# A hybrid encoder step: expert picks turned later and two more tiles whole, keys rotated before they are scaled, two reorderings in the front

## The chip, the cores and the metric

The kernel runs on one core of one Trainium2 chip. It is one program of 33,129 instructions on five engines: TensorE (PE; its weight loads are listed apart as PEld), VectorE (DVE), ScalarE (ACT), GpSimd (POOL) and SyncE (SP, which here only issues transfers). The metric is the device time of one execution in microseconds (us). Lower is better.

## The reference, cut to what matters

One layer for 384 tokens: one prompt of 256, and eight samples of 16 tokens each. What the change touches is the query and key part of the sparse attention and the expert layer.

```python
def _dsa(P_dsa, pos, k_pos, cache_k, cache_v, cache_kidx, q_norm_w, k_norm_w):
    q, k, v, qi, ki, wi = _split(P_dsa, [ATT_W, ATT_W, ATT_W, IDX_HEADS * IDX_DIM, IDX_DIM, IDX_HEADS])
    q = _rope(_rmsnorm(hs(q), q_norm_w), pos)        # 16 heads of 64
    k = _rope(_rmsnorm(hs(k), k_norm_w), pos)
    ...
    o = _sparse_attend(q, qi, wi, pos, k_all, v_all, ki_all, k_pos)

def _peer(h, w_pq, peer_keys, peer_u, peer_v):       # 16384 experts, 128 x 128 keys
    q = (hb @ w_pq).reshape(PEER_BLOCK, PEER_HEADS, 2, PEER_DHALF)
    s = einsum('nhpd,hpkd->nhpk', q, peer_keys)
    s1, i1 = top_k(s[:, :, 0], 16);  s2, i2 = top_k(s[:, :, 1], 16)
    sc, j = top_k(s1[..., :, None] + s2[..., None, :], 16)     # 16 experts per head and token
    g = softmax(sc)
    act = gelu(einsum('nhkd,nd->nhk', peer_u[e], hb))
    return einsum('nhk,nhkd->nd', g * act, peer_v[e])
```

Around these stand a modulation of the layer by a matrix `w_ada`, an RWKV branch with a state per head, two gates, and projections. All is float32.

## The kernel before

The program is written in the order of its stages, and a scheduler that runs when the program is built then sets one fixed order of instructions for each engine, from its own estimate of durations; on the chip each engine goes through its list in order and waits at the semaphores that stand in it. Another edit of the program can so move instructions far from the edit.

**The front (0 to about 718 us).** After the modulation's head and the norm, `run` goes through the letters of `ORDER`: R is a pair of RWKV heads (`rwkv_pair`, a long chain of small steps on all engines, among them y L845 to L676), M a unit of the modulation matrix (`mod_unit`: two loads of 512 KB of `w_ada`, 8 matmuls of full width), G a unit of the gates (`gate_unit`), D a quarter of the attention (`dsa_quarter`: keys, queries and values of four heads, attention of the samples in `attend_s` and of the prompt in `attend_p`). M and G are the filling for the chains of R and D on PE. The weights that need float32 precision are split in two rounded parts, `wh` by ACT (L230) and `wl` by DVE (L234), and multiplied in three matmuls.

In a quarter, `nat3` copies the 128x768 keys (then queries) out of PSUM to `qx`, ACT squares them (L947, into the buffer `rpt`), DVE sums (L949), `rstd` takes the power on POOL (L436), DVE scales `qx` in place (L951), and `rope` rotates: two half-size multiplies on POOL into `rpt` (L877, L878), one full-size multiply and one add on DVE into `qr` (L880, L881). Then PE turns the result (L959), and the key result is also written out (L955). `index` calls the same `rope` three times. PSUM has eight banks: `mm` two, `fx` two, `dx` two, `bx` and `cp` one each. All of `attend_p` is in the two `dx` banks.

**The mix (708 to 840 us)** reads the two branches back from DRAM into the tiles `px` (L1171), which take over memory of the front, splits them into `pbh` and `pbl` and multiplies.

**The experts' front (842 to 1290 us).** `peer_select` makes the picks of three groups of 128 tokens on DVE: group 0 for the sparse way, groups 1 and 2 for the dense way. At its end for groups 1 and 2, three transposes of the picks `pix` and the weights `pg` go to one `dx` bank (L1384) and are copied to `pT1`, `pT2`. In the same time PE goes through the tiles of `peer_u` in `dense_u`: the first `N1` of 128 unsplit, in float32 (8 matmuls of 256 columns, each of which the trace shows as two), in turn in the `mm` and `fx` banks; the tiles after those split, with 24 matmuls each. The sparse way (`peer_sparse`) gathers 1 MB a round (L1573, a ring of three buffers) and computes on DVE with the result (raw L1580, then acc L1586, with two small steps on ACT between); `pull` sets how many rounds are written beside a tile. `weights` takes `pT1`, `pT2` apart into digits (L1424 to L1427), makes one-hot factors on DVE and ACT, and multiplies them on PE (`mm<-oh`).

**Dense v (1290 to 1757 us)** multiplies with all of `peer_v`, loaded once.

## Time and profile before

| | us |
|---|---|
| median of 3 runs | 1762.96 |
| lowest, highest | 1759.18, 1770.17 |
| the profiled execution's own time | 1759.49 |
| its span, first to last instruction | 1757.7 |
| mean granted clock of PE | 0.981 |

The span is what all rows of the trace add up to; the profiled execution's own time has 1.8 us around it, and the median lies 3.5 us above that execution. A share of busy time is the mean over stages that are limited by different things, so a stage is read from its own window.

### The profile page before, as it was taken

What the parts mean: (1) busy time and instruction counts of PE and PEld (TensorE: products, weight loads), DVE (VectorE), ACT (ScalarE), POOL (GpSimd) and SP (SyncE); (2) the same over time, 40 slices, a digit from 0 to 9 for tenths busy, and PEclk for the clock granted to TensorE, in tenths of its full rate; (3) what the DMA queues carried; (4) which work ended last, traced back from release to release, by engine and by line L of the source; (5) the groups of instructions that cost most, each with busy time, mean ns of one, the idle gap of its engine ahead of it and who ended that gap; (6) DMA issues with size and microseconds to landing.
All of it is one profiled execution on the core that took longest, in us unless ns stands there. A gap on an engine that the chain in (4) does not pass through costs nothing.

```text
span 1757.7 us, 33129 instructions
## 1 busy us (share of the span) xinstructions
PE 1679.5 (96%) x12392; PEld 1410.2 (80%) x12392; DVE 1353.6 (77%) x2907; ACT 747.5 (43%) x1666; POOL 550.5 (31%) x616
## 2 busy tenths in 40 slices
PE   6999899999999999999998999999999999999998
PEld 4988788777888877899887889999976667767766
DVE  4448878778867765556999998899957778778787
ACT  4533343334342333335323255578853433443344
POOL 2433343333333421024032233342243224323232
PEclk8999899999999999999999999999999999999999
DMA  8543662555365365765488999997569999999996
GB/s 305 161 123 101 187 194 68 145 166 174 94 197 161 94 207 189 246 193 171 144 334 313 358 333 366 397 340 238 179 251 381 348 346 376 375 349 391 349 379 216
DMA packets 172537, 436.71 MB, mean 248 GB/s; under 512 B 46036, under 2 KB 86100, under 8 KB 155992
## 3 DMA queue, kind: packets, MB, share of 16 engines
q1 hardware_dynamic: 153944, 300.36, 50.8%
q0 software_dynamic: 18432, 134.23, 19.7%
q8 instruction: 98, 1.61, 0.4%
q14 instruction: 63, 0.52, 0.1%
HBM read 403.23 MB, written 31.30 MB: 247 GB/s over the span
## 4 chain that ended last, share of the span: by engine, by line
PE 55%; DVE 19%; DMA 11%; issue 8%; ACT 3%; POOL 2%; SPq 1%; DVEq 0%; POOLq 0%; ACTq 0%
PE mm L226 21%; PE fx L226 10%; PE dx L226 10%; PE cp L226 6%; PE bx L226 6%; DMA raw<-in_puv,pe 3%; DVE wl L234 3%; DVE raw L1580 2%; DVE acc L1586 2%; DMA w<-in_puT 2%; DMA w<-in_pv 2%; ACT wh L230 1%; DMA w<-in_w_in 1%; DVE TX L698 1%; DMA NL<-d 1%
## 5 line engine op out<-in xcount | busy, mean ns | idle before, releaser
L234 DVE TENSOR_TENSOR wl<-w,wh 128x1024 fp32r<-128x1024 f32 (+1 forms) x276 | 345.8, 1260 | 109.0 <-ACT wh L230 71.3
L230 ACT ACTIVATE wh<-w 128x1024 fp32r<-128x1024 f32 (+1 forms) x284 | 296.6, 1050 | 163.7 <-PE mm L226 74.3
L1573 POOL DMA_INDIRECT raw<-in_puv,pe x128 | 173.6, 1356 | 423.4 <-PE dx L226 155.4
L226 PE MATMUL fx<-h2h,wl 128*128 128x256 f32 x704 | 200.1, 285 | 8.2 <-DVE wl L234 8.0
L226 PE MATMUL fx<-h2h,wh 128*128 128x256 f32 x704 | 200.6, 285 | 1.4 <-ACT wh L230 1.1
L226 PE MATMUL fx<-h2l,wh 128*128 128x256 f32 x704 | 197.4, 281 | 0.0
L1586 DVE SCALAR_TENSOR_TENSOR acc<-raw,dots,acc 128x1024 f32<-128x1024 f32 x127 | 166.1, 1308 | 14.8 <-ACT dots L1582 14.8
L1580 DVE SCALAR_TENSOR_TENSOR raw<-raw,sh 128x1024 f32<-128x1024 f32 x128 | 158.9, 1241 | 14.0 <-DMA raw<-in_puv,pe 13.8
L226 PEld LDWEIGHTS fx<-h2h,wl 128*128 128x128 f32 x704 | 132.7, 189 | 12.3 <-DVE wl L234 11.5
L226 PEld LDWEIGHTS fx<-h2h,wh 128*128 128x128 f32 x704 | 132.6, 188 | 6.4 <-ACT wh L230 3.6
L226 PEld LDWEIGHTS fx<-h2l,wh 128*128 128x128 f32 x704 | 132.9, 189 | 1.6 <-issue 1.1
L226 PE MATMUL mm<-LTh,wh 128*128 128x384 f32 (+2 forms) x352 | 123.4, 351 | 1.4 <-ACT wh L230 0.8
L226 PE MATMUL mm<-LTl,wh 128*128 128x384 f32 (+2 forms) x352 | 123.1, 350 | 0.9 <-POOL LTl L488 0.9
L226 PE MATMUL mm<-LTh,wl 128*128 128x384 f32 (+2 forms) x352 | 122.4, 348 | 0.0
L226 PE MATMUL mm<-h2f,w 128*128 128x256 f32 x448 | 104.0, 385 | 0.0
L226 PE MATMUL mm<-wh,LTh 128*128 128x256 f32 x336 | 100.3, 299 | 2.9 <-ACT qx L888 2.9
L1581 ACT ACTIVATE dots<-dots 128x1 f32<-128x1 f32 x128 | 25.6, 200 | 177.0 <-DVE raw L1580 176.5
L226 PE MATMUL mm<-wl,LTh 128*128 128x256 f32 x336 | 99.4, 296 | 0.0
L226 PE MATMUL mm<-wh,LTl 128*128 128x256 f32 x336 | 98.6, 293 | 0.0
L226 PEld LDWEIGHTS mm<-h2f,w 128*128 128x128 f32 x448 | 85.0, 192 | 12.2 <-issue 0.2
L226 PE MATMUL fx<-h2f,w 128*128 128x256 f32 x320 | 73.8, 383 | 0.0
L226 PEld LDWEIGHTS mm<-LTh,wh 128*128 128x128 f32 (+2 forms) x352 | 66.5, 189 | 7.1 <-issue 3.0
(577 smaller groups left out, 4235.0 us busy)
## 6 DMA issues: line engine op xcount, KB each, us to landing
w<-in_puT SPq DMA_DIRECT2D x128, 512.0 KB, 7.1
w<-in_pv SPq DMA_DIRECT2D x128, 512.0 KB, 6.6
w<-in_w_in SPq DMA_DIRECT2D x70, 512.0 KB, 4.5
w<-in_w_ada SPq DMA_DIRECT2D x48, 512.0 KB, 4.8
cKT<-in_cKT SPq DMA_DIRECT2D x32, 256.0 KB, 4.3
cV<-in_cV SPq DMA_DIRECT2D x32, 256.0 KB, 4.5
w<-in_w_pq SPq DMA_DIRECT2D x16, 512.0 KB, 4.2
d<-wst SPq DMA_DIRECT2D x8, 832.0 KB, 4.3
```

What stands on the lines that cost most here:

```text
L226: return self.nc.tensor.matmul(out, l, r, start=start, stop=stop, skip_group_check=True, **kw)
L230: self.nc.scalar.activation(hi, src, AF.Copy)
L234: (self.nc.vector if eng == "v" else self.nc.gpsimd).tensor_tensor(lo, src, hi, op=OP.subtract)
L698: nc.vector.tensor_tensor(X[:, :t, :t], T[:, :t, :t].rearrange("p s c -> p c s"), NL[:, :t, t].unsqueeze(1).to_broadcast([48, t, t]), op=O ...
L1573: d = nc.gpsimd.indirect_dma_start(out=bass.AP(tensor=u.tensor, offset=u.offset, ap=[u.ap[0], [1, 2048]]), out_offset=None, in_=self.I["puv"],
L1580: nc.vector.scalar_tensor_tensor(u, u, 1.0, h2, op0=OP.mult, op1=OP.mult, accum_out=dot)
L1581: nc.scalar.activation(dot, dot, AF.Gelu_apprx_tanh)
L1586: nc.vector.scalar_tensor_tensor(acc, v, dot, acc, op0=OP.mult, op1=OP.add)
```

## The change

- **Turns.** `peer_select` returns the picks of groups 1 and 2, and a new function `turn` does the transposes. It is called after the loop of unsplit tiles, inside `issue_after(self.ulast.ins)`, which lets the scheduler place its instructions only behind the last unsplit tile's last matmul. The transposes go to the `bx` and `cp` banks, one each.
- **N1** goes from 40 to 42: two more `u` tiles unsplit, two fewer split. `pull` starts at tile 30 in the loop of unsplit tiles, so one more sparse round is written there.
- **Keys and queries.** `qx` is not scaled before the rotation; the squares go to the buffer `qr`, and the scale is multiplied into `qr` after the rotation. The second half-size multiply of `rope` goes from POOL to DVE.
- **ORDER.** The last twelve letters change from GDMMMGGGMGGM to GDMGMGMGMGGM.
- **The last quarter's `attend_p`** puts its transposes in `fx`, its products in `cp` and its last turn in `bx` in place of `dx`; the scores stay in `dx`.

```diff
-ORDER = "GGIggggR1R23DMMMGRMRDMRGMGMRMDGMMRRMGDMMMGGGMGGM"
-N1, NW, NA, NB = 40, 76, 8, 24
+ORDER = "GGIggggR1R23DMMMGRMRDMRGMGMRMDGMMRRMGDMGMGMGMGGM"
+N1, NW, NA, NB = 42, 76, 8, 24
...
         nc.gpsimd.tensor_tensor(t[:, :, :, 0:32], x[:, :, :, 32:64], B(2), op=OP.mult)
-        nc.gpsimd.tensor_tensor(t[:, :, :, 32:64], x[:, :, :, 0:32], B(3), op=OP.mult)
+        nc.vector.tensor_tensor(t[:, :, :, 32:64], x[:, :, :, 0:32], B(3), op=OP.mult)
...
-            sq = self.t([128, 3, 256], tag="rpt")
-            nc.scalar.activation(sq, x, AF.Square)
+            kr = self.t([128, 3, 4, 64], tag="qr")
+            nc.scalar.activation(kr.rearrange("p i a b -> p i (a b)"), x, AF.Square)
             ss = self.t([128, 3, 4], tag="qss", bufs=2)
-            nc.vector.tensor_reduce(out=ss, in_=H(sq), op=OP.add, axis=AX.X)
+            nc.vector.tensor_reduce(out=ss, in_=kr, op=OP.add, axis=AX.X)
             r = self.rstd(ss, ss, 1.0 / 64, EPS)
-            nc.vector.tensor_tensor(H(x), H(x), r.unsqueeze(3).to_broadcast([128, 3, 4, 64]), op=OP.mult)
-            kr = self.t([128, 3, 4, 64], tag="qr")
             self.rope(kr, H(x), 1 + which, 4)
+            nc.vector.tensor_tensor(kr, kr, r.unsqueeze(3).to_broadcast([128, 3, 4, 64]), op=OP.mult)
...
+        tags = ("fx", "cp", "bx") if u == 3 else 3 * ("dx",)
...
-            pv = self.ps([128, 4, 64], tag="dx")
+            pv = self.ps([128, 4, 64], tag=tags[1])
...
-                pt = self.ps([128, 2, 2, 128], tag="dx")
+                pt = self.ps([128, 2, 2, 128], tag=tags[0])
...
-            p = self.ps([128, 2, 128], tag="dx")
+            p = self.ps([128, 2, 128], tag=tags[2])
...
-        p = self.ps([128, 3, 128], tag="dx")
+        return idx, gw
+
+    def turn(self, i, idx, gw):
+
+        nc = self.nc
+        p = self.ps([128, 3, 128], tag=("bx", "cp")[i - 1])
         for q, src in enumerate((idx[:, 0].rearrange("p h k -> p (h k)"), idx[:, 1].rearrange("p h k -> p (h k)"), gw)):
...
-                self.mm(p, u[:, k], self.h2f[:, k], start=(k == 0), stop=(k == 7))
+                self.ulast = self.mm(p, u[:, k], self.h2f[:, k], start=(k == 0), stop=(k == 7))
...
+        with self.tc.issue_after(self.ulast.ins):
+            T = [None] + [self.turn(i, *T[i]) for i in (1, 2)]
```

How the order moves, at three places (names end in buffer numbers; x8 is eight of the kind in a row).

PE in the kernel before, at the end of the unsplit tiles: `h2f` is the activations, `w` a tile of `peer_u`, `dx` the bank of the second turn.

```order
L1384 MATMUL dx_11297<-cfirst,pix_11259 128x128
L226 MATMUL mm_11752<-h2f_9800,w_11750 128x256 x8
L226 MATMUL fx_11771<-h2f_9800,w_11769 128x256 x8
L226 MATMUL mm_11783<-h2f_9800,w_11781 128x256 x5
L1384 MATMUL dx_11297<-cfirst,pix_11259 128x128
L1384 MATMUL dx_11297<-cfirst,pg_2219_11290 128x128
L226 MATMUL mm_11783<-h2f_9800,w_11781 128x256 x3
L226 MATMUL fx_11802<-h2f_9800,w_11800 128x256 x8
L226 MATMUL mm_11814<-h2f_9800,w_11812 128x256 x8
L226 MATMUL mm_13141<-oh_13138 128x128 x4
L226 MATMUL bx_13155<-oh_13148 128x128 x4
L226 MATMUL mm_13207<-oh_13204 128x128 x4
```

PE in the changed kernel, at the same place; `h2h`, `h2l`, `wh`, `wl` are the split parts.

```order
L226 MATMUL fx_11813<-h2f_9792,w_11811 128x256 x8
L226 MATMUL mm_11825<-h2f_9792,w_11823 128x256 x8
L1389 MATMUL bx_11842<-cfirst,pix_11015 128x128 x2
L1389 MATMUL bx_11842<-cfirst,pg_2161_11046 128x128
L1389 MATMUL cp_11848<-cfirst,pix_11245 128x128 x2
L1389 MATMUL cp_11848<-cfirst,pg_2209_11276 128x128
L226 MATMUL fx_11868<-h2h_11854,wh_11869 128x256
L226 MATMUL fx_11868<-h2l_11855,wh_11869 128x256
L226 MATMUL fx_11900<-h2h_11854,wh_11901 128x256
L226 MATMUL fx_11900<-h2l_11855,wh_11901 128x256
L226 MATMUL fx_11868<-h2h_11854,wl_11870 128x256
```

The turns now stand in one block behind the tiles, the second turn's first transpose no longer ahead of the last five tiles, and the one-hot matmuls that stood ahead of the first split tile are gone from here (they come after three split tiles).

DVE in the kernel before, from the last reduction of the picks (`pix`) on; `raw` and `acc` are the sparse rounds, `wA` the first step of the digits.

```order
L1365 TENSOR_REDUCE pix_11259<-poh_11283 128x64
L1586 SCALAR_TENSOR_TENSOR acc_11699<-raw_13330,dots_13332,acc_11699 128x1024
L1580 SCALAR_TENSOR_TENSOR raw_13397,dots_13399<-raw_13397,sh_2290_11697 128x1024
L1586 SCALAR_TENSOR_TENSOR acc_11699<-raw_13397,dots_13399,acc_11699 128x1024
L1424 CAST wA_13126<-pT_2172_11065 128x128
L1448 TENSOR_TENSOR oh_13138<-pT_2172_11065,dx_13124 128x512
L1425 TENSOR_SCALAR wA_13126<-wA_13126 128x128
L1426 CAST wab_13127<-wA_13126 128x128
L1580 SCALAR_TENSOR_TENSOR raw_13470,dots_13472<-raw_13470,sh_2290_11697 128x1024
```

DVE in the changed kernel, from the same reduction on (the digits and the first `wl` are in the four rows behind).

```order
L1365 TENSOR_REDUCE pix_11245<-poh_11269 128x64
L1585 SCALAR_TENSOR_TENSOR raw_13215,dots_13217<-raw_13215,sh_2278_11677 128x1024
L1591 SCALAR_TENSOR_TENSOR acc_11679<-raw_13215,dots_13217,acc_11679 128x1024
L1585 SCALAR_TENSOR_TENSOR raw_13282,dots_13284<-raw_13282,sh_2278_11677 128x1024
L1591 SCALAR_TENSOR_TENSOR acc_11679<-raw_13282,dots_13284,acc_11679 128x1024
L1585 SCALAR_TENSOR_TENSOR raw_13349,dots_13351<-raw_13349,sh_2278_11677 128x1024
L1591 SCALAR_TENSOR_TENSOR acc_11679<-raw_13349,dots_13351,acc_11679 128x1024
L1585 SCALAR_TENSOR_TENSOR raw_13422,dots_13424<-raw_13422,sh_2278_11677 128x1024
L1591 SCALAR_TENSOR_TENSOR acc_11679<-raw_13422,dots_13424,acc_11679 128x1024
L1585 SCALAR_TENSOR_TENSOR raw_13488,dots_13490<-raw_13488,sh_2278_11677 128x1024
L1591 SCALAR_TENSOR_TENSOR acc_11679<-raw_13488,dots_13490,acc_11679 128x1024
L1585 SCALAR_TENSOR_TENSOR raw_13555,dots_13557<-raw_13555,sh_2278_11677 128x1024
```

Before, two more `raw` (26 in all up to the reduction) stand ahead of the picks' end and the digits follow after one more; now 24 stand ahead of it, and then six `raw` and five `acc` stand between the picks' end and the digits, with the first `wl` right behind.

PE in the kernel before, at the last attention's second half (`se` are its exponentials, `vv` the values) and the first products of the mix (`mm<-pbh`).

```order
L1092 MATMUL dx_8813<-cfirst,se_8801 128x128 x4
L226 MATMUL dx_8812<-vv_8202,set_8818 128x64 x4
L1092 MATMUL dx_8824<-cfirst,se_8809 128x128 x4
L226 MATMUL mm_9145<-pbh_9114,wh_9134 128x384
L226 MATMUL mm_9172<-pbh_9114,wh_9134 128x384
L226 MATMUL mm_9145<-pbl_9115,wh_9134 128x384
L226 MATMUL mm_9145<-pbh_9114,wl_9135 128x384
L226 MATMUL mm_9145<-pbh_9114,wh_9134 128x384
L226 MATMUL mm_9145<-pbl_9115,wh_9134 128x384
L226 MATMUL mm_9145<-pbh_9114,wl_9135 128x384
L226 MATMUL mm_9172<-pbl_9115,wh_9134 128x384
```

PE in the changed kernel, at the same place.

```order
L1092 MATMUL fx_8805<-cfirst,se_8793 128x128 x2
L674 MATMUL bx_8133<-cfirst,y_7931 128x128 x3
L226 MATMUL cp_8759<-vv_8196,set_8770 128x64 x2
L1092 MATMUL fx_8805<-cfirst,se_8793 128x128 x2
L1105 MATMUL bx_8777<-cfirst,ob_8775 128x128 x2
L1092 MATMUL fx_8816<-cfirst,se_8801 128x128 x2
L226 MATMUL cp_8804<-vv_8196,set_8810 128x64 x4
L1092 MATMUL fx_8816<-cfirst,se_8801 128x128 x2
L226 MATMUL cp_8804<-vv_8196,set_8821 128x64 x4
L1105 MATMUL bx_8830<-cfirst,ob_8828 128x128 x2
L226 MATMUL mm_9137<-pbh_9106,wh_9126 128x384
L226 MATMUL mm_9164<-pbh_9106,wh_9126 128x384
```

The whole attention now stands ahead of the first product of the mix; before, its last two steps stood in between the products, 14 and 25 rows behind the first.

## Rows read from the trace of the kernel before

**Rows 1.** Page of the kernel before, part 1: engine, busy us, share, instructions.

```profile
PE 1679.5 (96%) x12392; PEld 1410.2 (80%) x12392; DVE 1353.6 (77%) x2907; ACT 747.5 (43%) x1666; POOL 550.5 (31%) x616
```

**Rows 2.** Windows of 20 us: length, busy (instructions) per engine, clock, DMA.

```profile
180.00:200.00 20.00, 16.59 (x148) 14.57 (x147) 18.04 (x53) 6.90 (x18) 10.38 (x10) 0.93 0.46 144
300.00:320.00 20.00, 17.45 (x209) 15.88 (x210) 15.09 (x39) 5.33 (x12) 6.59 (x9) 0.83 0.38 101
700.00:720.00 20.00, 16.21 (x71) 13.36 (x71) 8.31 (x13) 7.14 (x16) 0.00 (x0) 0.73 0.70 238
940.00:960.00 20.00, 17.10 (x76) 14.17 (x77) 20.00 (x66) 6.73 (x17) 7.57 (x4) 0.83 0.71 263
1060.00:1080.00 20.00, 18.42 (x160) 18.22 (x159) 16.32 (x18) 8.29 (x18) 7.90 (x5) 1.00 1.00 381
1140.00:1160.00 20.00, 19.93 (x173) 19.74 (x172) 19.99 (x26) 16.11 (x42) 10.83 (x8) 1.00 0.95 361
```

**Rows 3.** Waits of PE, 160 to 720 us: total, times, longest.

```profile
PE dx L959 <- DVE qr L881: 3.4, 1, 3.4
PE mm L226 <- ACT qx L888: 2.9, 2, 1.9
...
PE mm L226 <- DMA w<-in_w_ada: 2.2, 1, 2.2
```

**Rows 4.** Timeline of PE round both turns: start, length, instruction [idle <-releaser].

```profile
942.90 0.45 PE L1384 MATMUL dx<-cfirst,pix 128*128 128x128 f32 x1 [4.87 <-DVE pix L1365]
...
983.23 3.62 PE L226 MATMUL mm<-h2f,w 128*128 128x256 f32 x16
986.68 3.62 PE L226 MATMUL fx<-h2f,w 128*128 128x256 f32 x16
...
1012.98 0.30 PE L1384 MATMUL dx<-cfirst,pix 128*128 128x128 f32 x1 [1.95 <-DVE pix L1365]
...
1030.72 1.13 PE L226 MATMUL mm<-oh 128*128 128x128 f32 x8
...
1035.31 0.39 PE L226 MATMUL fx<-h2h,wl 128*128 128x256 f32 x1 [1.42 <-DVE wl L234]
```

**Rows 5.** Timeline of DVE from the end of the picks to the first wl.

```profile
1019.72 1.08 DVE L1365 TENSOR_REDUCE pix<-poh 128x64 f32<-128x256 bf16 x2
...
1023.74 1.28 DVE L1586 SCALAR_TENSOR_TENSOR acc<-raw,dots,acc 128x1024 f32<-128x1024 f32 x1 [0.60 <-ACT dots L1582]
...
1027.21 0.29 DVE L1427 SCALAR_TENSOR_TENSOR wab<-wab,pT 128x128 bf16<-128x128 bf16 x1
...
1034.03 1.23 DVE L234 TENSOR_TENSOR wl<-w,wh 128x1024 fp32r<-128x1024 f32 x1
```

**Rows 6.** Issues of line L1573 (gathers), 900 to 1150 us.

```profile
DMA to landing us min/median/max: 5.7/9.1/11.3
```

**Rows 7.** Timeline of the last attention's end, SP queue and ACT.

```profile
695.08 0.32 SPq L676 DMA_DIRECT2D d<-sq  x1
...
703.78 0.80 SPq L1171 DMA_DIRECT2D px<-d  x2
...
707.18 0.84 ACT L230 ACTIVATE pbh<-px 128x768 fp32r<-128x768 f32 x1 [1.42 <-DMA px<-d]
```

**Rows 8.** Timeline of POOL in a rotation.

```profile
174.81 1.30 POOL L877 TENSOR_TENSOR rpt<-qx,rt 128x384 f32<-128x384 f32 x1 [4.09 <-DVE qx L951]
...
176.07 1.71 POOL L878 TENSOR_TENSOR rpt<-qx,rt 128x384 f32<-128x384 f32 x1
```

**Rows 9.** Timeline of DVE and POOL in two other rotations.

```profile
328.86 1.10 POOL L877 TENSOR_TENSOR rpt<-qx,rt 128x384 f32<-128x384 f32 x1 [0.60 <-DVE qx L951]
...
329.02 1.74 DVE L880 TENSOR_TENSOR qr<-qx,rt 128x768 f32<-128x768 f32 x1
...
603.27 1.02 POOL L877 TENSOR_TENSOR rpt<-qx,rt 128x384 f32<-128x384 f32 x1 [1.62 <-DVE qx L951]
...
603.92 1.19 DVE L880 TENSOR_TENSOR qr<-qx,rt 128x768 f32<-128x768 f32 x1 [0.46 <-DMA d<-qr]
```

## The prediction

> **What bounds the kernel now.** I read the page's busy shares first, then the kernel in windows of 20 us with the granted clock beside the busy time, then who makes PE wait, and last the timeline at each place that the change touches. PE is busy for 1679.5 of 1757.7 us [rows 1], so some 78 us of PE idle time is all that can be taken away without taking PE work away, beside the time at a low clock. The windows show where these are. At 180, 300, 700 and 940 us PE is idle for 2.5 to 3.8 of 20 us and the clock is 0.93, 0.83, 0.73 and 0.83 [rows 2]. A granted clock of 0.83 says that 17% of a window's matmul time was lost to the lower of the two levels, 3.4 us of 20, on top of the idle time. From 1060 us on PE is nearly full, and beside it the transfers (share 1.00 at 1060) or DVE (19.99 of 20 at 1140) [rows 2]: there three engines are near their limit at once, and a gain on one of them is soon caught by the next.
>
> **The turns, and 42 tiles.** Before, PE waits 4.87 us and 1.95 us in front of a turn's first transpose, until DVE has the picks; with the slow matmuls after the first wait (clock 0.83, 3.4 us) that is 10.2 us [rows 2, 4]. The change takes both away: the transposes stand behind the last unsplit tile. In place of them come two unsplit tiles of 3.45 us (983.23 to 986.68) [rows 4], 6.9 us. The unsplit tiles ended at 1030.72 [rows 4], where the first one-hot matmul starts; they now end near 1030.72 - 10.2 + 6.9 = 1027.4, and with six transposes and four first matmuls of split tiles PE is through at about 1029.
>
> What is late next is the first `wl`. DVE sets it, and it was full in this stretch (20.00 of 20) [rows 2], so the waits of PE were a symptom and not the limit. Before, the first `wl` starts at 1034.03, behind 29 `raw` and 28 `acc`, and ahead of it stood the rest of the digits and the first factors and one-hots: from 1027.21 to 1034.03, 6.8 us, of which one `raw` and one `acc` took 2.4, so 4.4 us. These now follow the first `wl`; in return the order has one round more ahead of it (30 and 29), 2.4 us. If DVE never sat idle, the first `wl` would so start at 1034.03 - 4.4 + 2.4 = 1032.0. But the six rounds behind the picks stand alone: each `acc` waits for two ACT steps, 0.60 us as at 1023.74 [rows 5], five times, 3.0 us; and each gather takes 9.1 us to land in the median [rows 6] with three buffers, so a round comes at the earliest every third of 9.1 + 2.4 + 0.6, 4 us, of which DVE works 2.4. Two or three rounds lie ready when the picks end, the others may wait up to 1.6 us each. I take 1035 for the start of the first `wl` (between 1032 and 1037), and 1036.2 for PE's start on it, against 1035.31 before [rows 4, 5]. PE then sits idle for about 7 us, longer than the 4.87 us after which the clock fell before, so I charge the same 3.4 us for slow matmuls.
>
> The sum for PE: 0.9 later at the first `wl`; two split tiles fewer behind it, 48 matmuls at 19.93/173 = 0.115 us [rows 2], -5.5; the 24 one-hot matmuls that used to fill the hole, now behind it, +2.8; slow matmuls +3.4. That is +1.6. If `wl` comes at 1032 and the clock stays, it is -4.9; with 1037, +2.6. DVE has two `wl` fewer (1.23 each [rows 5]), -2.4, and idles some 3 us more. I take **-1** with ends -5 and +3: the two long waits go, and most of it is given back one row further on.
>
> **The last attention.** Before, the second half's scores, transposes, products and turns go through two `dx` banks one after the other. The memory of `px` comes free only when the front's last reads are done, its transfer is issued at 703.78 and `pbh` starts at 707.18 [rows 7], PE's first product of the mix behind it. The other way to `px` is the write of `sq` into the branch's buffer, issued at 695.08 [rows 7]. With its transposes and products in other banks the second half's scores stand before the first half's products, so `px` could be issued when `sq` has landed, at about 698.5, if that write takes the 3.4 us that `px` itself took: up to 5.3 us earlier. Two groups of attention work (about 2 us of matmuls), which ran in the mix's own waits before, now stand ahead of the products. The window's 3.8 us of idle time and clock of 0.73 (5.4 us) [rows 2] are the most that can go: -9; nothing, if the RWKV chain in front of `sq` is the limit, 0. I take **-4**, near what the earlier transfer gives less the moved work.
>
> **Modulation order.** One wait of 2.2 us for `w_ada` [rows 3] stands in the stretch that the letters change; with G units (512 KB for 24 matmuls) between M units (1 MB for 8), it should go. **-1.5**, ends -2.2 and +1.
>
> **Keys and queries.** The path from `qx` to the turned keys held a scale, then on POOL 1.30 and 1.71 us in series (174.81 to 177.8) [rows 8], then the add. Now POOL has one multiply, DVE does the other beside it (0.6 us, half of a full-size one's 1.19 [rows 9]), and both can run while the power is taken on POOL's queue or before; only the scale waits for it. The path is some 3 to 4 us shorter. What PE lost to it: 3.4 + 2.9 us in three waits [rows 3], and slow matmuls in windows 180 and 300, 1.4 + 3.4 us [rows 2]; 11 us at most. The price: 10 half-size multiplies on DVE, 6 us, in windows where DVE has 2 to 5 us free of 20 [rows 2], hidden where it is not the releaser. The new wait: the squares go to `qr`, which the writes of keys (L955) and of the attention's result read, so ACT can stand in front of a square until that transfer is done, with all splits of weights (`wh`) and copies out of PSUM queued behind it, and PE behind those. No row shows that wait. I take **-3**, with ends -11 and +8.
>
> On the pair POOL and DVE the rows don't agree with each other: one 128x768 rotation multiply took 1.74 us while POOL worked beside it, another 1.19 us, beside POOL's multiply of 603.27 [rows 9]. The Trainium skill, page "SBUF — State Buffer", section "Who interferes with whom", says that a VectorE instruction with two inputs in SBUF and a GpSimd instruction that reads SBUF exclude each other, which speaks against a half-size multiply on each at one time. By that rule the two halves would run in series again, about the rival below.
>
> **Sum.** -1 -4 -1.5 -3 = -9.5 on a profiled execution of 1759.5: 1750. The median stands 3.5 us above that execution, so **1753**.
>
> **Rivals.**
> *All front waits go.* Turn -5, attention -9, modulation -2.2, keys -9: 1759.5 - 25 + 3.5 = 1738. For it speaks that each of these waits has a row; against it, that after a removed wait the same engine mostly waits for the next thing in the chain, and that the scheduler lays the whole front anew.
> *The hole only moves.* First `wl` at 1037 behind the sparse rounds, the attention bound by the RWKV chain (-2), keys and modulation at nothing: 1759.5 + 3 - 2 + 3.5 = 1764. For it: DVE full in 940 to 960, transfers full at 1060 [rows 2].
> *POOL and DVE in series.* If the DVE half waits for POOL's (1.10 us, as at 328.86 beside the slow row at 329.02 [rows 9]), DVE pays up to 10 times that, 11 us, in the quarters; half of it shows, keys cost +3 in place of -3: 1759.
> *Slower: squares held by the buffer `qr`.* Seven of the eight squares come behind a write that reads `qr`. One hold that makes PE wait as long as in the window at 300 costs what that window lost, 2.55 us idle and 3.4 us of clock, 6 us. Seven of them are 42 us, against the -6.5 of the other parts: 1759.5 + 35.5 + 3.5 = 1798. It decides from four such holds on. Against it: between the keys and the queries stand three groups of 24 matmuls, some 8 us at 0.115, about as long as the keys' own path to the write, so the write should have begun before the squares are due.
>
> **How the numbers follow.** Forecast 0.50, all waits go 0.16, hole moves 0.22, in series 0.07, squares held 0.05. A measurement here can tell about 1%, 17.6 us: faster means below 1745.3, slower above 1780.6. Faster holds all of the second case and the lower part of the forecast's own spread (0.10 of its 0.50), 0.26; slower is the last case, 0.05; the rest, 0.69, lies within 1%. The range reaches from 1738, the second case's time, to 1768, the third case with its sparse rounds at their worst; it leaves out half of the second case, the last one, and a little more.
>
> **What would show it.** Right: no wait of PE for `pix`; unsplit tiles without a break to about 1028; a wait of 4 to 8 us for the first `wl`, after it a window with a clock below 1; `px` issued before 700 if the front ends as before; no waits of PE for `qx` or `qr` over 2 us. Wrong: a first `wl` before 1031 relative to the mix's start as now, which would bring the turn's full 9 us; ACT idle at its squares, released by a transfer; new waits of PE of over 3 us anywhere before 700 us, since the front's order is all new.

## The result, and the profile after

The changed kernel takes 1774.08 us in the median of 9 runs (1767.59 to 1781.68), the kernel before 1764.25 in 9 runs on the same chip (1759.12 to 1770.17). The ratio is 1.0057, with an interval of 1.0039 to 1.0075: slower by 10 us, where 9.5 us less were forecast, and above the range. All ratios here leave out two executions that ran at a granted clock of 0.838 and 0.555; the second was the profiled one of the kernel with 38 tiles below, so no trace of that kernel is read. The profiled execution took 1774.75 us, with a span of 1773.0. That of before lay 4.8 us under the median of its 9 runs, so the two spans differ by 15.3 us where the kernels differ by 10.

Page of the changed kernel, part 1, in the columns of [rows 1].

```profile
PE 1687.3 (95%) x12376; PEld 1413.9 (80%) x12376; DVE 1358.4 (77%) x2916; ACT 745.8 (42%) x1664; POOL 528.2 (30%) x605
```

PE has 16 instructions fewer than before and is busy 7.8 us longer [rows 1]. By the prediction's own prices the two unsplit tiles take 1.4 us more than the 48 split matmuls that they replace; the mean granted clock, 0.978 against 0.981, makes some 5 us of the rest. The windows of the changed kernel say where (three of [rows 2], and 1040 to 1060).

```profile
300.00:320.00 20.00, 18.66 (x200) 16.84 (x199) 15.35 (x37) 5.84 (x12) 6.55 (x7) 0.83 0.36 93
700.00:720.00 20.00, 16.43 (x82) 14.35 (x80) 10.29 (x22) 7.88 (x21) 2.29 (x2) 0.74 0.63 217
940.00:960.00 20.00, 15.48 (x63) 12.71 (x62) 16.32 (x66) 5.29 (x12) 4.52 (x6) 0.89 0.94 356
...
1040.00:1060.00 20.00, 16.69 (x124) 16.11 (x125) 19.25 (x29) 12.93 (x31) 4.29 (x3) 0.83 0.92 334
```

The window at 700 is as it was, 16.43 us of PE at a clock of 0.74 against 16.21 at 0.73 [rows 2]. At 940 PE is now idle for longer than before, 4.5 us against 2.9. At 1040 there is a new slow window, 0.83. Timeline of PE in the changed kernel round both places.

```profile
956.50 6.68 PE L226 MATMUL fx<-h2f,w 128*128 128x256 f32 x16 [4.35 <-ACT G L1494]
...
1032.08 3.62 PE L226 MATMUL mm<-h2f,w 128*128 128x256 f32 x16
1035.54 0.38 PE L1389 MATMUL bx<-cfirst,pix 128*128 128x128 f32 x2
...
1041.57 0.58 PE L226 MATMUL fx<-h2h,wh 128*128 128x256 f32 x1 [5.21 <-ACT wh L230]
...
1044.08 0.58 PE L226 MATMUL fx<-h2h,wh 128*128 128x256 f32 x1 [1.71 <-ACT wh L230]
...
1044.90 0.58 PE L226 MATMUL fx<-h2h,wl 128*128 128x256 f32 x1
```

No turn waits for `pix` any more, and the six turns follow the last unsplit tile without a break. In place of the wait of 4.87 us for `pix` [rows 4] stands one of 4.35 us at 956.50, for a Gelu, and the tile behind it takes 6.68 us where one at full clock takes 3.62. Behind the turns PE waits 5.21 and 1.71 us, and its first `wl` is at 1044.90, where before it was at 1035.31 [rows 4]. Timeline of DVE in the changed kernel there.

```profile
1020.94 1.09 DVE L1365 TENSOR_REDUCE pix<-poh 128x64 f32<-128x256 bf16 x2
1021.94 1.22 DVE L1585 SCALAR_TENSOR_TENSOR raw<-raw,sh 128x1024 f32<-128x1024 f32 x1
...
1025.67 1.23 DVE L1585 SCALAR_TENSOR_TENSOR raw<-raw,sh 128x1024 f32<-128x1024 f32 x1 [0.62 <-DMA raw<-in_puv,pe]
...
1037.74 1.22 DVE L1585 SCALAR_TENSOR_TENSOR raw<-raw,sh 128x1024 f32<-128x1024 f32 x1 [0.74 <-DMA raw<-in_puv,pe]
...
1041.61 1.23 DVE L1585 SCALAR_TENSOR_TENSOR raw<-raw,sh 128x1024 f32<-128x1024 f32 x1 [0.75 <-DMA raw<-in_puv,pe]
...
1043.63 1.21 DVE L234 TENSOR_TENSOR wl<-w,wh 128x1024 fp32r<-128x1024 f32 x1
```

Between the picks' end and the first `wl` stand the six rounds that the order showed. Every one but the first waits for its gather, and they come 3.7 to 4.3 us apart. Timeline of ACT in the changed kernel in both places.

```profile
952.60 0.20 ACT L1586 ACTIVATE dots<-dots 128x1 f32<-128x1 f32 x1 [4.22 <-DVE raw L1585]
...
953.14 1.28 ACT L1369 ACT_TABLE_LOAD   x1
954.44 0.31 ACT L1369 ACTIVATE pg<-pg 128x128 f32<-128x128 f32 x1
954.77 1.28 ACT L1494 ACT_TABLE_LOAD   x1
956.06 0.38 ACT L1494 ACTIVATE G<-fx 128x256 f32<-128x256 f32 x1
...
1039.01 0.20 ACT L1586 ACTIVATE dots<-dots 128x1 f32<-128x1 f32 x1 [2.78 <-DVE raw L1585]
...
1039.71 0.48 ACT L1391 ACTIVATE pT<-bx 128x384 f32<-128x384 f32 x1
...
1040.45 1.06 ACT L230 ACTIVATE wh<-w 128x1024 fp32r<-128x1024 f32 x1
```

ACT goes through its list in order, and the small step of a round (`dots`) stands in it. At 952.60 it holds up the Gelu for which PE waits: 4.22 us for `raw`, then two table loads of 1.28 us round an exponential. At 1039.01 it holds up the copies of the turns and the first `wh`. So the hole behind the turns is the rounds' pace, passed on by ACT.

The front, in the changed kernel: the only wait of PE for `qx` or `qr` from 160 to 720 us, then the SP queue, then the wait of ACT for a DMA that the change brings.

```profile
PE dx L958 <- DVE qr L952: 0.5, 1, 0.5
```

```profile
706.00 0.33 SPq L676 DMA_DIRECT2D d<-sq  x1
707.99 0.80 SPq L1171 DMA_DIRECT2D px<-d  x2
```

```profile
ACT qr L947 <- DMA d<-qr: 3.5, 2, 2.7
```

The waits for `qx` and `qr` fell from 6.3 [rows 3] to 0.5 us. PE still waits for `w_ada`, 2.8 us in two parts, but not at the old place. The wait of before stood at 643.67 us, where the letters change, and is gone; the two new ones stand at 195 and 198 us, where before PE waited 3.4 us for `qr`. Timeline of PE in the kernel before, then in the changed one:

```profile
197.75 0.85 PE L959 MATMUL dx<-cfirst,qr 128*128 128x128 f32 x6 [3.41 <-DVE qr L881]
...
643.67 0.64 PE L226 MATMUL mm<-w,cst 128*32 128x256 f32 x8 [2.19 <-DMA w<-in_w_ada]
```

```profile
195.29 0.64 PE L226 MATMUL mm<-w,cst 128*32 128x256 f32 x8 [1.22 <-DMA w<-in_w_ada]
...
197.55 0.76 PE L226 MATMUL mm<-w,cst 128*32 128x256 f32 x8 [1.62 <-DMA w<-in_w_ada]
```

`sq` is written at 706.00, where it was at 695.08 [rows 7], so `px` comes 4.2 us later and not earlier.

From the timelines of PE and DVE, the span divides as in this table (each from one execution; the stage of `u` goes from the first matmul with a `u` tile to the last row of one-hot matmuls; all points are starts of rows).

| us | before | after |
|---|---|---|
| first matmul of a `u` tile | 842.0 | 843.8 |
| from there to the last unsplit tile's last row | 185.2 | 188.3 |
| to the first `wl` on DVE | 192.0 | 199.8 |
| to the last row of one-hot matmuls | 449.2 | 460.1 |
| from that row to the last matmul | 461.3 | 463.9 |
| PE idle: to the picks' end, from there to the first `wl` on PE, from there to the last one-hot row | 6.8, 1.4, 7.3 | 4.5, 7.0, 12.6 |

Time less idle time is 433.7 us before and 436.0 after, and 428 to 436 in all the traces read here: the stage is PE's work, which hardly changes, and PE's waits. It grew by 10.9 us, 8.6 of it waits of PE: 5.6 us more in the hole and 5.3 more behind it, where nothing was forecast, less 2.3 up to the picks' end.

### The profile page after: what moved, and what is told of

It reads as the page before. It is cut to its first block, busy times and chain, and to the rows that moved or that the text cites. A ratio compares the mean times of both kernels' runs of the same rounds, so it can differ in the third digit from the quotient of the medians.

```text
span 1773.0 us, 33100 instructions
## 1 busy us (share of the span) xinstructions
PE 1687.3 (95%) x12376; PEld 1413.9 (80%) x12376; DVE 1358.4 (77%) x2916; ACT 745.8 (42%) x1664; POOL 528.2 (30%) x605
## 4 chain that ended last, share of the span: by engine, by line
PE 56%; DVE 19%; DMA 13%; issue 5%; ACT 4%; POOL 1%; SPq 1%; DVEq 0%; ACTq 0%; POOLq 0%
PE mm L226 22%; PE dx L226 10%; PE fx L226 10%; PE cp L226 7%; PE bx L226 6%; DMA raw<-in_puv,pe 4%; DVE wl L234 3%; DVE raw L1585 2%; DVE acc L1591 2%; DMA w<-in_w_in 2%; DMA w<-in_puT 2%; ACT wh L230 2%; DMA w<-in_pv 1%; DVE TX L698 1%; DMA w<-in_w_ada 1%
## 5 line engine op out<-in xcount | busy, mean ns | idle before, releaser
L1578 POOL DMA_INDIRECT raw<-in_puv,pe x128 | 167.0, 1305 | 445.3 <-PE dx L226 158.3
L226 PE MATMUL fx<-h2h,wh 128*128 128x256 f32 x688 | 198.7, 289 | 10.8 <-ACT wh L230 8.0
L226 PEld LDWEIGHTS fx<-h2h,wh 128*128 128x128 f32 x688 | 131.8, 192 | 15.5 <-ACT wh L230 10.1
L226 PEld LDWEIGHTS fx<-h2h,wl 128*128 128x128 f32 x688 | 131.8, 192 | 10.1 <-DVE wl L234 9.6
L226 PE MATMUL fx<-h2f,w 128*128 128x256 f32 x336 | 79.7, 391 | 4.3 <-ACT G L1494 4.3
L226 PEld LDWEIGHTS mm<-LTh,wh 128*128 128x128 f32 (+2 forms) x352 | 67.3, 191 | 15.3 <-ACT wh L230 5.0
```

The costliest lines, as they stand in the source:

```text
L226: return self.nc.tensor.matmul(out, l, r, start=start, stop=stop, skip_group_check=True, **kw)
L1578: d = nc.gpsimd.indirect_dma_start(out=bass.AP(tensor=u.tensor, offset=u.offset, ap=[u.ap[0], [1, 2048]]), out_offset=None, in_=self.I["puv"],
```

## The experiments

I began with two theories: that the hole behind the turns makes the loss (**the hole**), and that the new front loses it (**the front**). Each run was compared with the kernel before on its own chip, which took 1762.6 to 1765.7 us in the median.

**The change in halves.** The first kernel has the turns and 42 tiles and the front of before; the second has the keys, `ORDER` and the attention's banks alone. Edit of the second against the changed kernel:

```diff
-N1, NW, NA, NB = 42, 76, 8, 24
+N1, NW, NA, NB = 40, 76, 8, 24
...
-        with self.tc.issue_after(self.ulast.ins):
-            T = [None] + [self.turn(i, *T[i]) for i in (1, 2)]
```

> The kernel before with the turns behind the last unsplit tile and N1 at 42, the front untouched. Theory A (the loss lies at the turns: PE's waits for the picks are gone, but the first wl stands behind six sparse rounds that come one every 3.95 us, so PE waits some 7 us with slow matmuls behind it, and the gap stays to the end): slower than before by 6 to 11 us, ratio 1.0035 to 1.006, the hole in front of the first split tile 5 us or more. Rival B (the loss lies in the front, whose chain ends later): ratio 0.998 to 1.001.

> The kernel before with the three edits of the front (keys and queries, ORDER, the last attention's banks), turns and N1 as before. Theory A: the front ends 1 to 2 us later, as in the changed kernel (first unsplit tile at 843.8 against 842.0), and the whole is slower by 0 to 3 us, ratio 1.000 to 1.002. Rival B: slower by 6 to 11 us, ratio 1.0035 to 1.006.

Measured: 1.0054 [1.0031, 1.0077] and 1.0010 [0.9994, 1.0027]. The turns with the tiles are 9.5 us slower alone, nearly all of the loss, and the front is no faster. In the first one's profile the hole is there:

```profile
PE fx L226 <- ACT wh L230: 7.8, 2, 5.9
```

**Turns and tiles apart.** Turns with 40 tiles, 42 tiles with the turns of before, and 38 tiles.

```diff
-N1, NW, NA, NB = 40, 76, 8, 24
+N1, NW, NA, NB = 42, 76, 8, 24
```

> The turns behind the last unsplit tile, N1 left at 40. Its order has four sparse rounds between the picks' end and the first wl, not six. Theory A: the picks end near 1021, the first wl starts near 1036 to 1038 while the unsplit tiles end near 1027, so the hole is longer than with 42 tiles, 8 to 11 us; time 4 to 10 us above before, ratio 1.002 to 1.006. Rival B: ratio 0.998 to 1.001. If the two tiles are what costs, this one is faster than before by 3 us or more.

> N1 at 42 alone, turns as before (two waits of PE for the picks, transposes in the dx bank). Two split tiles fewer on PE (5.5 us) and DVE (2.4 us), two unsplit more (6.9 us). Theory A: the waits for the picks stay, the first wl comes some 2 to 6 us later without a hole of over 3 us, and the time is within 3 us of before, ratio 0.998 to 1.002. If the two tiles are what costs, slower by over 4 us.

> The kernel before with N1 at 38: two unsplit tiles fewer and two split ones more. 42 alone was 1.0042. If the count of unsplit tiles has a slope of its own (PE 0.7 us a tile, the first split tile and one-hots behind them): 0.996 to 0.999, the last one-hot at 446 to 448. If 40 is where the tiles meet the picks' end: 1.000 to 1.004.

Measured: turns alone 1.0042 [1.0021, 1.0062], 42 tiles alone 1.0042 [1.0022, 1.0062], 38 tiles 1.0008 [0.9989, 1.0028]. Each costs about 7.4 us, and together 9.5. Whether they share a part isn't shown: the sum of the two, 14.8 us, and the 9.5 lie 5.3 us apart, and each of the three has an interval of some 4 us to either side. The theory of the hole had 0.998 to 1.002 for the two tiles alone and missed: they were not the small change that I had taken them for. With 38 tiles nothing is won either, so the count of tiles has no plain slope.

**The turns two tiles earlier.** With 42 tiles, the turns stand behind the 40th, with two unsplit tiles left for PE.

```diff
+TURN = {39: [1, 2]}
...
+            if j in TURN:
+                with self.tc.issue_after(self.ulast.ins):
+                    for i in TURN[j]:
+                        T[i] = self.turn(i, *T[i])
```

> As the kernel with turns and 42 tiles alone, but the turns stand behind the 40th unsplit tile, so that two tiles run on PE while the picks are turned and taken apart; its order has four sparse rounds, not six, between the picks' end and the digits, and six one-hot steps of DVE ahead of the first wl. Theory C (the stage up to the last one-hot is set by DVE: its length was 427 us plus DVE's idle time in all six traces so far, 22.0 us idle before and 31.1 with the turns at the end; what PE waits for doesn't count): DVE idles some 26 us, the last one-hot comes 451 to 454 us behind the first u tile (449.2 before, 456.1 with the turns at the end), ratio to before 1.001 to 1.003. Theory A (PE's hole in front of the first split tile is what costs): the hole falls under 3 us, and the time is 0.996 to 1.000 of before.

Measured: 1.0051 [1.0024, 1.0077], the same as the first kernel. The first `wl` came 198.7 us after the first tile, as in the changed kernel (199.8) and no sooner than in the first kernel (196.9): 30 rounds still stood ahead of it. The hole stayed too, 7.7 us from the picks' end to the first `wl`, now in front of the first one-hot, so this run doesn't test what the hole costs. The last one-hot came at 453.0 us, as the theory of DVE had it, but the time did not fall with it (1.0051, where 1.001 to 1.003 was expected).

**Is DVE's load what sets the stage?** DVE is full for long stretches, so I tried it from two sides. In the kernel before, eight tiles multiply with `wh` in place of `wl` and DVE leaves out eight subtractions of 1.23 us; so that kernel leaves out the low part of eight tiles' weights and counts the rounded part twice. In the other, every eighth `wl` of `u` is on POOL.

```diff
+NOLO = (44, 48, 52, 56, 60, 64, 68, 72)
...
-            uh, ul = (x.rearrange("p (k e) -> p k e", k=8) for x in self.split(u, UENG[j % len(UENG)]))
+            if j in NOLO:
...
+                self.nc.scalar.activation(uh, u, AF.Copy)
+                uh = ul = uh.rearrange("p (k e) -> p k e", k=8)
+            else:
...
```

```diff
-UENG, VENG, GENG, VN = 'v', 'v', 'g', 3
+UENG, VENG, GENG, VN = 'vvvvvvvg', 'v', 'g', 3
```

> The kernel before, with DVE's subtraction left out for eight of the split u tiles (tiles 44 to 72, every fourth): the rounded part wh is used in the place of wl, so PE and ACT do the same work and the output lacks these corrections. DVE has 8 x 1.23 = 9.8 us less. Theory C: the last one-hot comes 7 to 10 us sooner behind the first u tile, and the time is 0.994 to 0.997 of before. Theory A, or a stage set by PE: ratio 0.998 to 1.001.

> The kernel before, with every eighth wl of the split u tiles made by POOL in place of DVE (2.4 us each there, 1.23 on DVE; four or five of these tiles come before the last one-hot, eleven in all). Theory C: DVE has 5 to 6 us less up to the last one-hot, which comes 3 to 6 us sooner; ratio 0.996 to 0.999, if POOL's queue, where the gathers are issued, does not give it back. Theory A: 0.999 to 1.002.

Measured: 1.0008 [0.9990, 1.0027] and 1.0064 [1.0038, 1.0089]. Windows of the kernel before, then of the one without the eight subtractions, 1060 to 1280 us:

```profile
1060.00:1280.00 220.00, 215.01 (x1836) 212.61 (x1834) 203.11 (x259) 151.98 (x374) 71.38 (x52) 1.00 0.81 299
```

```profile
1060.00:1280.00 220.00, 214.68 (x1839) 211.85 (x1839) 194.86 (x253) 151.23 (x370) 66.02 (x51) 1.00 0.81 302
```

DVE loses 8.25 us of work there, PE does the same 215 us, and the last one-hot comes at 450.1 us (449.2): in the kernel before, DVE's load is not the limit. The kernels with the turns moved were not tried so. With a `wl` on POOL, it takes 2.4 us or more instead of 1.2, PE's waits for `wl` of DVE grow from 5.5 to 9.2 us over the stage, and the kernel is slower by 11 us.

**The rounds held back.** If the six rounds make the hole, then a gather that waits for the last unsplit tile should take it away. With the turns behind the last of 42 tiles the 27th round's gather waits, with the turns behind the 40th the 26th, and with 40 tiles the 26th.

```diff
-                if self.pace is not None:
+                pace = self.ulast.ins.name if j == 26 and q == 0 else self.pace
+                if pace is not None:
```

> As the kernel with turns and 42 tiles alone, but the gather of the 27th sparse round waits for the last unsplit tile (its semaphore stands on POOL's queue), so that 26 rounds and not 30 stand ahead of the digits and the first wl; the computation is the same. Theory A (the rounds ahead of the first wl, one every 3.95 us, make PE's hole, and PE's waits add up to the stage's length): the first wl comes 186 to 190 us behind the first u tile (196.9 without the wait), the hole is 2 to 4 us, the last one-hot comes at 449 to 452 (456.1), ratio to before 0.999 to 1.002. Rival E (the four rounds only move: they hold up DVE behind, and PE with it): the hole is gone, but the last one-hot stays at 454 to 457, ratio 1.003 to 1.006.

> Turns behind the 40th of 42 unsplit tiles, and the gather of the 26th sparse round waits for that tile: 25 rounds stand ahead of the digits, and the order has three one-hot products right behind the last unsplit tile, ahead of the first split one, as in the kernel before. No hole and an early first one-hot at once. Theory F (the stage's end follows the time of the first one-hot, since 64 groups of them have to go through DVE, ACT, PE and back beside a fixed list of tiles and rounds; the hole alone doesn't matter): the first one-hot product 185 to 190 us behind the first u tile (188.7 before, 207.9 with the turns at the end, 201.5 with 26 rounds), the last one at 447 to 451, ratio 0.998 to 1.002. Rival E (the sparse rounds that are put off hold up the stage later): the last one-hot at 453 to 457, ratio 1.003 to 1.006.

> Turns behind the last of 40 unsplit tiles, and the gather of the 26th sparse round waits for that tile: as the kernel with the turns and 40 tiles alone (1.0042, hole 9.7 us), with 25 and not 28 rounds ahead of the first wl. If what was left over with 42 tiles and no hole (1.0025) comes from the number of tiles (42 alone: 1.0042): 0.998 to 1.001, the first wl 181 to 185 us behind the first u tile, the last one-hot at 447 to 450. If it comes from the turns' place: 1.002 to 1.004, the last one-hot at 452 to 456 with PE waiting for one-hots in the last 40 us of the stage.

Measured: 1.0033 [1.0017, 1.0050], 1.0025 [1.0001, 1.0050] and 1.0037 [1.0016, 1.0057]. No hole of over 2.3 us is left in front of the first `wl` in any of them. Timeline of PE behind the turns in the first of them:

```profile
1030.96 0.27 PE L1389 MATMUL cp<-cfirst,pg 128*128 128x128 f32 x1
1032.81 0.38 PE L226 MATMUL fx<-h2h,wh 128*128 128x256 f32 x1 [1.58 <-ACT wh L230]
```

The wait is 1.58 us where it was 5.21 in the changed kernel, and the matmul takes 0.38 us where it took 0.58. But against the kernels without the pace only 3.7, 4.6 and 0.9 us come back, and each of these differences has an interval of 5 to 6 us to either side. The stage still lasts 455.6, 454.9 and 453.6 us, where without the pace it lasted 456.1, 453.0 and 454.9. PE's idle time from the picks' end to the first `wl` is now 2.3, 0.0 and 2.0 us (8.5, 7.7 and 10.6 without the pace), and behind it 17.2, 16.8 and 19.4 (11.6, 11.4 and 10.2; 7.3 in the kernel before). In the second kernel a wait of 3.14 us for `wh` stands 16 us further on, and the matmuls behind it take 0.41 us in place of 0.28. Waits of PE from 1060 to 1320 us, in the kernel before (the first rows), then in the last of these kernels:

```profile
PE fx L226 <- DVE wl L234: 4.1, 6, 1.6
PE cp L226 <- ACT oh L1453: 1.0, 1, 1.0
...
PE mm L226 <- DVE oh L1401: 0.4, 1, 0.4
```

```profile
PE fx L226 <- DVE wl L234: 4.6, 7, 1.2
PE mm L226 <- DVE oh L1406: 3.5, 2, 2.1
PE cp L226 <- ACT oh L1458: 2.5, 4, 1.6
PE mm L226 <- DVE oh L1453: 1.6, 2, 0.8
PE mm L226 <- ACT oh L1458: 1.3, 1, 1.3
```

The waits for `wl` are nearly the same; those for the one-hots are 8.9 us in place of 2.1. So the theory of the hole falls: when the hole goes, waits of PE further on take its place, about half of them for one-hots, and no gain from it is clear of the noise. The first kernel, at 455.6 us and 1.0033, did as the rival in its expectation says; the forecast for an early first one-hot (447 to 451) missed too; and with 40 tiles it came as expected if the turns' place is what costs.

**Do the rounds that were put off come back later?** Four rounds, the 26th to the 29th, are left out, in the paced kernel with the turns behind the 40th tile and in the kernel before. Both kernels so leave four of the 128 rounds of experts out of the result; in the paced one the next round's gather waits.

```diff
+                if q == 0 and 25 <= j < 29:
+                    yield
+                    continue
```

> The kernel of the last run (turns behind the 40th of 42 tiles, 25 rounds ahead of the digits) with four sparse rounds, 25 to 28, left out altogether (no gather, no raw, no acc; the output lacks four of 128 picks' experts). Nothing ahead of the first wl differs, and behind it DVE has 4 x 2.45 = 9.8 us less, ACT's two small steps per round and four gathers fewer. Theory E (the rounds that were put off hold up the split tiles behind, through ACT's small steps that wait for them): PE's idle time between the first wl and the last one-hot falls from 16.8 to 8 to 12 us, and the last one-hot comes at 447 to 451 us (454.9 with the rounds). If the rounds don't matter: 453 to 457. The total falls in any case by some 2.7 us for each MB that is not gathered in the later stage, if that stage is limited by transfers: ratio 0.990 to 0.996.

> The control: the kernel before with the same four sparse rounds left out (the output lacks them too). Its order ahead of the first wl stays (29 rounds, now other ones), and four rounds fewer stand behind. Theory E: there PE is hardly held up by rounds (7.3 us idle in that stretch), so the last one-hot comes at 446 to 450 (449.2), a smaller fall than in the other. If each round costs the stage the same in both kernels, the two fall alike, by 4 to 10 us. Total 0.990 to 0.995.

Measured: 1.0009 [0.9988, 1.0030] and 0.9937 [0.9908, 0.9967]. The kernel before gains 11 us from it; the paced one goes only from 1.0025 to 1.0009. In the stage itself both became shorter by about the same, 5.4 and 4.5 us (the paced one to 449.5, inside the theory's 447 to 451). From 1060 to 1320 us PE's waits for one-hots fall from 7.8 to 2.4 us in the paced kernel, and from 2.1 to nothing in the other. So the rounds do hold up the one-hots, but they do so in both kernels: that putting them off is what sets the two apart isn't supported, since the stages still lie 4.9 us apart (5.7 with all rounds). The totals were forecast at 0.990 to 0.996 and 0.990 to 0.995; the paced kernel's missed that.

**The front's parts.** The attention's banks, the keys and `ORDER`, each alone in the kernel before, and the first two together.

```diff
-ORDER = "GGIggggR1R23DMMMGRMRDMRGMGMRMDGMMRRMGDMMMGGGMGGM"
+ORDER = "GGIggggR1R23DMMMGRMRDMRGMGMRMDGMMRRMGDMGMGMGMGGM"
```

> The last attention's banks alone. The three edits of the front came to 1.001 together. If this edit gives the 4 us that were forecast and the others take them back: 0.997 to 0.9985, with px issued before 702. If the RWKV chain in front of the write of sq sets the end: 0.999 to 1.001, px issued at the time of that write's end whatever the attention does.

> Keys and queries alone: the scale behind the rotation, the squares in the buffer qr, the second half-size multiply on DVE. The last attention's banks alone were 0.9971, all three edits of the front 1.0010, so keys and ORDER together cost some 0.4%. If the keys cost it: 1.002 to 1.005, with new waits of PE, or of ACT at the squares, that before doesn't have. If not: 0.997 to 1.000 (the forecast of 3 us gained was 0.998).

> The new ORDER alone. If it costs what keys and ORDER cost together: 1.002 to 1.005, the chain in front of the write of sq ending later (706 in the changed kernel, 695 to 703 in those with the old ORDER) while the fillers end at the same time. If not: 0.998 to 1.001.

> The last attention's banks and the keys together, ORDER, turns and N1 as before. Alone they came to 0.9971 and 0.9986. If they add up and the new ORDER is what takes the gain away in the three together (1.0010): 0.994 to 0.998. If they don't go together: 0.999 to 1.002, with the write of sq after 703.

Measured: attention 0.9971 [0.9949, 0.9993], keys 0.9986 [0.9962, 1.0011], `ORDER` 1.0013 [0.9993, 1.0033] (between its two forecasts), attention and keys 0.9980 [0.9961, 0.9999]. SP queue of the kernel with the attention's banks alone, then of the one with all three parts:

```profile
697.77 0.32 SPq L676 DMA_DIRECT2D d<-sq  x1
700.43 0.80 SPq L1172 DMA_DIRECT2D px<-d  x2
```

```profile
706.21 0.33 SPq L676 DMA_DIRECT2D d<-sq  x1
708.21 0.80 SPq L1171 DMA_DIRECT2D px<-d  x2
```

With the banks alone `px` is issued 2.7 us behind the write of `sq`, where it was 8.7 behind [rows 7]. With the new `ORDER` the write of `sq` itself is at 706.21, and with `ORDER` alone it is at 704.41: there PE's last matmul for a G unit is at 685.9 us and for an M unit at 689.9, before at 686.9 and 689.3. So the filling ends where it did, and the last RWKV pair ends later. With the attention and the keys together the write is at 699.97 and `px` at 701.94, and the ratio lies inside the 0.994 to 0.998 that was expected if the parts add up, at its upper end.

**The best parts together.** The attention's banks with the paced turns of 42 tiles.

> The last attention's banks, the turns, 42 tiles and the wait of the 27th gather together, keys and ORDER as before. If the parts add up: 0.9971 times what the kernel with the wait gives, 0.996 to 0.999 by theory A, 1.000 to 1.003 by rival E.

Measured: 1.0046 [1.0025, 1.0066]. This is above both forecasts, and above the 1.0004 that the two parts would give if they added up, by 0.0042 with an interval of some 0.0035. The front is early there, `px` at 701.81 and the first `u` tile at 837.5 us, and the stage of `u` is the longest of those with the turns moved, 460.3 us with 20.0 of PE's waits behind the first `wl`. So the attention's gain is lost here without the new `ORDER`, and why is open. The paced turns stay a loss with the attention's banks beside them, and the best version is the kernel before with the attention's banks alone: 1756.55 us against 1762.62, 0.3% faster than the kernel before.

## Why the prediction was wrong

**The turns: the term -1 with ends -5 and +3 failed.** Measured alone it is +9.5 us [+5.5, +13.6]. Its mechanism was the right one up to the first `wl`: the waits for `pix` went, the six rounds stand behind the picks, and PE waits about 7 us in front of the first split tiles, at a clock that then falls to 0.83 as charged. Three sizes in it were off, one was missing, and the sum was read too low: PE's own rows came to +1.6, and -1 was taken by setting DVE's -2.4 against them, though PE was the engine that waits. With a `wl` at 1037 that sum is +3.6 and not +2.6.

- *The first `wl`, 1035 at most 1037.* It came at 1043.63, or 7.8 us later than before if both are counted from the first `u` tile. I let two or three gathers lie ready at the picks' end; five of six rounds waited for theirs, 0.62 to 1.17 us each. The pace of 4 us a round that I worked out was right, and held from the first round on; from the picks' end at 1020.8 [rows 5] it puts the sixth `raw` at 1041, where it came (1041.61). That DVE was full was read from 940 to 960 us [rows 2], 80 us ahead of this place. The picks' end did not move earlier in this execution (178.2 us after the first tile, 178.8 before).
- *The gain at the first turn, 4.87 us and 3.4.* A wait for a Gelu took its place, 4.35 us, and the tile behind it lost 3.1 us to the clock (6.68 - 3.62). ACT stood between DVE's rounds and PE; I had looked at DVE as the engine that is late and at ACT only as 0.60 us within a round. In the profile of the first experiment PE's waits for Gelus from 840 to 1060 us come to 3.0 us, none over 1.1, so this wait is no part of every such kernel.
- *Two tiles for 48 split matmuls, 6.9 - 5.5.* Alone they cost 7.4 us and not 1.4.
- *Missing:* PE's waits behind the first `wl`, 12.6 us against 7.3. I took the rest of the stage as PE's work alone. The runs show that its work does stay about the same (428 to 436 us), and that the waits move: about half of them to the one-hots, when the hole is taken away.

**The rival "the hole only moves" was the nearest, and its price was too low.** It gave the turns +3. It has the right place for the first wait. But the loss is not the hole's price: with the hole taken away 0.9 to 4.6 us come back, none of it clear of the noise, and the stage stays as long.

**The last attention: right.** -4 was forecast, -5.1 us [-9.0, -1.2] measured alone, and by the step foretold: `px` at 700.43, 2.7 us behind the write of `sq`. What failed is that the sum added it to the other parts, beside which no gain was measured. The rival's condition "the attention bound by the RWKV chain" came true through `ORDER`.

**Modulation order: the term -1.5 failed.** `ORDER` alone is +2.3 us [-1.2, +5.8], not told apart from nothing, though the wait of 2.2 us for `w_ada` [rows 3] went as foretold: with `ORDER` alone PE has no wait for `w_ada` from 160 to 720 us. I had weighed only the wait and not what the letters do to the RWKV pair that runs beside them. The sum of the front's parts alone is -5.3 us; measured together they are +1.8 [-1.1, +4.8]. The two lie 7.1 us apart, with an interval of some 7.4, so it is only likely that they don't add up. With the write of `sq` at 706 `px` can't come early; that this is the whole of the difference is argued, not shown.

**Keys and queries: the size held.** -3 forecast, -2.5 us [-6.7, +1.9] measured, and PE's waits for it fell by 5.8 us. Of these 2.8 us came back at the same place as waits for `w_ada` (at 195 and 198 us; 2.5 us with the keys alone); the clock of the window at 300 stayed at 0.83, so that part of the 11 us didn't come back. The two rivals on it are both there, and small. *Squares held:* ACT waits twice for the write out of `qr`, 3.5 us in all, two holds where four were needed to decide. One of them reaches PE; timeline of ACT, DVE and PE in the changed kernel:

```profile
307.51 0.84 ACT L947 ACTIVATE qr<-qx 128x768 f32<-128x768 f32 x1 [2.73 <-DMA d<-qr]
...
308.39 0.95 DVE L949 TENSOR_REDUCE qss<-qr 128x12 f32<-128x768 f32 x1 [0.55 <-ACT qr L947]
...
310.30 0.33 PE L226 MATMUL cp<-Sb,NX 64*64 64x64 f32 x4 [1.34 <-DVE NX L782]
```

The step `NX` of the RWKV pair stands behind the sum of the squares on DVE. Its wait is 1.3 us in all four profiles with the new keys and 0.3 us in the kernel before, not the 6 us that the rival charged for a hold. *POOL and DVE in series:* in the changed kernel, timeline of POOL, then of DVE,

```profile
319.20 1.58 POOL L877 TENSOR_TENSOR rpt<-qx,rt 128x384 f32<-128x384 f32 x1 [4.68 <-ACT qx L888]
...
461.05 1.95 POOL L877 TENSOR_TENSOR rpt<-qx,rt 128x384 f32<-128x384 f32 x1 [2.42 <-ACT qx L888]
```

```profile
319.82 1.37 DVE L878 TENSOR_TENSOR rpt<-qx,rt 128x384 f32<-128x384 f32 x1
...
462.94 0.54 DVE L878 TENSOR_TENSOR rpt<-qx,rt 128x384 f32<-128x384 f32 x1
```

The DVE half that starts within POOL's ends 0.41 us behind it (321.19 against 320.78) and takes 1.37 us; one that starts at POOL's end takes 0.54. So DVE's half waited for POOL's. The Trainium skill, page "SBUF — State Buffer", section "Who interferes with whom", says so for two such instructions, and this trace agrees. But in the quarters DVE's half is longer in three of eight cases, by 0.63 to 0.83 us, 2.2 us of DVE time. The two halves in `index` are held up as well, by a `wl` on POOL and not by POOL's half; timeline of POOL and DVE in the changed kernel:

```profile
78.31 2.40 POOL L234 TENSOR_TENSOR wl<-w,wh 128x1024 fp32r<-128x1024 f32 x1 [4.14 <-ACT kiT L911]
...
78.75 2.38 DVE L878 TENSOR_TENSOR rpt<-qx,rt 128x384 f32<-128x384 f32 x1 [1.08 <-ACT qx L888]
```

This half again ends 0.42 us behind POOL's instruction (81.13 against 80.71); the other takes 2.48 us. In all the price was some 6 us of DVE time and not 11.

**What stays open.** With no hole and 40 tiles the turns still cost 6.5 us [2.8, 10.1]. In the eight profiles with the turns moved and all rounds the stage of `u` lasts 453.0 to 460.3 us; in seven with the turns of before and 40 tiles it lasts 446.7 to 450.6, the one with `wl` on POOL apart (461.6). What makes it is waits of PE: the hole and, behind it, waits for `wl`, Gelus and one-hots in the kernels without the pace, and for about half of it one-hots in the three paced ones. What sets these is not shown. The time of the first one-hot doesn't explain them: with the turns behind the 40th tile and paced, the first one-hot matmul is at 188.8 us of the stage as before (188.7), and the last still at 454.9. The rounds hold up one-hots, but four rounds fewer shorten the stage of the kernel before about as much. DVE's load was lightened by itself in the kernel before alone; in two of the paced kernels DVE is busy for 80.0 of 80 us from 1160 to 1240 us (79.0 before), and that it is the limit there was not tried. Why 42 tiles alone cost 7.4 us is open too: their stage is 3 us longer, and their profile has no long new wait. The scheduler lays the whole stage anew at each of these edits, and no edit here held the order of the rest fixed.

## What to carry to other kernels

When a wait for a late engine is moved out of the way, look at everything that the scheduler then puts between that engine and the next thing that PE needs, and follow it through the third engine: here rounds on DVE, each waiting for its gather, held ACT, and ACT held PE. And ask where the waits go when that one is taken away: here nearly all of the hole came back as waits further on. Price a pipeline of a few buffers at its steady pace from the first round, since nothing says that rounds lie ready. Parts of a front that all lead to one transfer need not add: the attention's gain of 5 us was real alone and was not to be seen beside a reordering that made another way to that transfer late, nor beside the paced turns, so parts are to be measured alone and together and the best kept.

## What the runs showed of the hardware

- An instruction of DVE with two inputs in SBUF and one of POOL hold each other up. DVE's half-size multiply takes 0.54 us alone; three that started within POOL's took 1.17 to 1.37 us, two that started within a `wl` of POOL 2.38 and 2.48, and each ended 0.41 or 0.42 us behind POOL's. It goes the other way as well: POOL's half, 1.01 us at best, took 1.95 us when it started within a `wl` of DVE, and 2.73 when a `wl` and the half of DVE both fell in its time.
- A wait of 4.35 us by PE was followed by a tile mostly at the lower of its two clock levels, 6.68 us for 16 matmuls in place of 3.62; a wait of 1.58 us was followed by matmuls at the higher one (0.38 us for the first, where 0.58 followed the wait of 5.21).
- An exponential between two Gelus costs ACT two table loads of 1.28 us, and both lay within a wait of PE of 4.35 us.
- The beginning of the experts, the first matmul with a `u` tile, lies between 836.8 and 848.0 us in the profiles of kernels whose code is the same up to there. One execution can't tell such a front's edits of 2 to 4 us; only the ratios over 9 to 13 runs did.
- To take 8.25 us of work from DVE, which was busy for 203 of 220 us, gave nothing in the kernel before.
